# Three halves of an up projection from plain products to seven block products, and sums of a later weight made earlier

## The chip, the cores and the metric

The kernel runs on one core of one Trainium2 chip. A core has TensorE (PE, matrix products), VectorE (DVE), ScalarE (ACT), GpSimd (POOL) and SyncE (SP), which run independently and wait for each other through semaphores. Transfers are issued in this kernel from two queues, SP's and POOL's; only POOL's can add to what lies at the destination. An engine works through its own instructions in order, so a waiting instruction holds back all behind it on that engine.

The metric is the device time of one execution in microseconds. Lower is better.

## The reference

One encoder layer over 512 tokens of width 2048, in float32:

```python
h = rms_norm(x, pre_mix_g)
z = h @ w_in                                   # [q | k | v | u], 1024 columns each
a = chunked_attention(q, k, v, rel_bias)       # 8 heads of 128
p = multiscale_pool(u, pool_w, pool_scale)     # 4 groups of 256, windows 2, 4, 8, 16
x = x + rms_norm(concat(a, p) @ w_o, post_mix_g)
h = rms_norm(x, pre_ffn_g)
up = causal_dwconv(h @ w_up, conv_w, conv_b)   # 2048 -> 2 x 5632, 3 taps over tokens
y = (gelu(up[:, :5632]) * up[:, 5632:]) @ w_down
x = x + rms_norm(y, post_ffn_g)
```

## The kernel before

**Products.** Every float32 operand is split in two parts of a shorter format, hi and lo (`split`, L133: ACT rounds, L135; DVE subtracts, L136), and a product is hi*hi + hi*lo + lo*hi: three matmuls with 128x512 operands (`mm3`, L150).

**Stages on PE**, with where they lie in the profiled execution: the heads' q, k and v and the attention (0 to 303 us); the *pool branch*, that is eight projections u0 to u7 of 128 channels each, with the trailing means (`pool_proj`, `pool_keep`, `pool_mix`; 303 to 406 us); the product with w_o, by seven block products instead of eight (`wo_product`; 406 to 564 us); the up projection (564 to 1443 us); the product with w_down, again by seven block products (to 1877 us). `pool_keep` (L485) clears small margins on POOL before DVE's additions over them.

**Up projection.** It is done in 22 units of 256 channels. A unit has two halves: p = 0 feeds the gelu (`gate`), p = 1 is the value that it is multiplied with (`product`, which stores g to DRAM by POOL's queue). The first `PLAIN` = 3 units are plain (`up`, L984): 16 blocks of the inner dimension, two of 128 channels, three matmuls each. The weights come in four tiles per half. Of these, the first unit is written out (its second half reads the tiles `w10_0` to `w10_3`).

From unit 3 on each half is a *pair* k = 0, 1, ... (k counts halves) of `seven` products P1 to P7 (L1185): the 2 x 2 blocks of channels and inner dimension, against the 2 x 2 blocks of inner dimension and tokens, by a scheme that needs seven block products for eight. A block product is `mm2` (L156): eight matmuls of 512 columns (hi of the weight against hi and lo of h) and eight of 256 (lo of the weight against hi of h). On the side of h, P1, P2, P4 and P7 read blocks of h where they lie (for P7 a block must first be overwritten by a difference: `h_difference`, L1056); P5, P6 and P3 read sums made by `h_sums` (L1033) into tiles h5, h6, h3. On the side of w_up, the factors of P5, P6 and P4 are made in one buffer `x` in turn, that of P7 in the buffer `y` of P3: after a factor is split, POOL's queue adds the next block of w_up to its buffer (`add`, L1100), and so on:

```python
if i == 1 and k not in self.alone:
    self.add(k, "x", 1, 0)
elif i == 5:
    self.add(k, "x", 1, 1)
elif i == 6:
    self.add(k, "x", 0, 1)
elif i == 3:
    self.add(k, "y", 1, 0)
```

P1 of a pair is split from `x` too before the first addition; only for the first and the last pair (`alone`) does it have a buffer `w` of its own, and `x` is loaded and added to separately. In the steady order two neighbouring pairs are interleaved: place 7 k + (0, 2, 4, 6, 8, 10, 12) for P1, P2, P5, P3, P6, P7, P4. The first and the last few products have an order of their own (`begin`, `end`). Factors are split up to four products ahead of PE (`AHEAD`; the tiles `w4` hold four hi and lo pairs, shared with the plain weights), and loaded up to six further (`RAW`). The buffers `x` lie in a ring of four (`raw_x`), which `h_sums` also uses for its temporaries, two of which live until `h_difference`. `raw4` is a ring of five for the other raw weights.

**Sums in DRAM.** Seven block products with w_o and w_down need sums of their blocks. `sums_in_dram` (L296) makes them with transfers from DRAM to DRAM: `copy` by SP's queue, behind the last weight load issued so far, and `add` by POOL's queue. It has 32 steps for w_o and then 16 for w_down (eight copies, eight adds, 1 MB each; tiles `t`); in w_down's, the sums come in the order 5, 7, 6, 4, where 6 starts as a copy of the finished 5 and 4 as a copy of the finished 6. The rest of the kernel takes single steps at places written out: 24 during the heads, eight in the pool branch, seven in `wo_product` and nine in `up`.

**Order.** The order of PE's instructions is the program's (`manual_schedule`). On the other engines and queues a planner places each instruction when the kernel is built, by its own estimates of when operands and buffers are ready, with earlier instructions of the program preferred; `issue_after(ins)` makes an instruction follow `ins` on the same engine. A tile name with `bufs=n` is a ring of n buffers; a new use waits until the old one is no longer read. PSUM is a ring of eight banks.

Of the kernel before, what the change touches and what calls it, by code (L numbers as in the profile page):

```python
# [75 lines left out]
def encoder_layer(ctx: ExitStack, tc: tile.TileContext, x, xT, vecs, rel, post_mix, post_ffn,  # L76
# [56 lines left out]
    def split(hi, lo, src, scale=None):  # L133
        if scale is None:
            rounded = nc.scalar.activation(hi, src, AF.Copy)  # L135
            rest = nc.vector.tensor_sub(lo, src, f32(hi))  # L136
        else:
            rounded = nc.scalar.activation(hi, src, AF.Copy, scale=scale)
            rest = nc.vector.scalar_tensor_tensor(lo, src, scale, f32(hi), op0=ALU.mult, op1=ALU.subtract)
        split.last, split.rest = rounded.ins, rest.ins  # L140
        return rounded.ins
# [138 lines left out]
    for i in WO:  # L280
        for cc in range(2):
            specs += wo_specs(i, cc)
        if i == 1:
            specs += pm_spec(3)
    for u in range(PLAIN):
        for p in range(2):
            specs += [(f"w{p}{u}_{i}", w_up[u, p, :, i // 2, :, i % 2 * 512:(i % 2 + 1) * 512].rearrange(
                "m p c -> p m c"), 2, 512) for i in range(4)]

# [69 lines left out]
    with tc.tile_pool(name="p1", bufs=2, reuse_waits="tile") as p1:  # L359
# [39 lines left out]
        def project(name, between=None):  # L399
            ps = bank(name)  # L400
            for i in range(2):
                if i and between:
                    between()
                w = weights.get(f"{name}_{i}")
                for j in range(8):
                    kb = 8 * i + j
                    mm3(ps, part(w, j), blk(hT, kb), kb == 0, kb == KD - 1)
            return ps
# [73 lines left out]
        def pool_proj(g, j):  # L482
            pool_keep(g, j, project(f"u{2 * g + j}"))
# [53 lines left out]
        for h in range(2, HEADS):  # L537
# [9 lines left out]
            else:  # L547
                values(h - 2)
            next(sums_step)
        next(sums_step)  # L550
        pool_proj(0, 0)
        turn(6)
        scores(7)
        pool_proj(0, 1)
        next(sums_step)
        values(6)
        next(sums_step)
        pool_proj(1, 0)
        next(sums_step)
        turn(7)  # L560
        pool_proj(1, 1)
        next(sums_step)
        values(7)
        mixT += [acc8(f"mixT{i}", "B").rearrange("p (a b) -> p a b", a=4) for i in (2, 3)]
        pool_mix(0, keep_mix)
        next(sums_step)
        pool_proj(2, 0)
        next(sums_step)
        pool_proj(2, 1)
        pool_mix(1, keep_mix)  # L570
        next(sums_step)
        pool_proj(3, 0)
        u7 = project("u7")


# [16 lines left out]
        def wo_product(i, cc, left, between=None):  # L592
            ps = [bank(f"m{i}{cc}{t}") for t in range(2)]
            if cc:
                next(sums_step)
            for q in range(4):
                w = weights.get(f"wo{i}_{cc}_{q}")
                for j in range(2):
                    kb = 2 * q + j
                    for t in range(2):  # L600
                        mm3(ps[t], tuple(v[:, kb, t * P:(t + 1) * P] for v in left), part(w, j), kb == 0, kb == 7)
                if between:
                    between(q)
            return ps
# [335 lines left out]
    with tc.tile_pool(name="p3", bufs=2, reuse_waits="tile") as p3:  # L940
# [37 lines left out]
        def normed(ps):  # L978
            z = new_z()
            for j in range(2):  # L980
                nc.vector.tensor_mul(z[:, j, :], ps[j], R)
            return z

        def up(u, p, between=()):  # L984
            ps = [bank(f"up{u}_{p}_{j}") for j in range(2)]
            between = list(between)
            for i in range(4):
                w = weights.get(f"w{p}{u}_{i}")
                factors.prefetch(4 - len(weights.specs) + weights.used)
                for kb in range(4 * i, 4 * i + 4):  # L990
                    for j in range(2):
                        mm3(ps[j], part(w, j, slice(kb % 4 * P, (kb % 4 + 1) * P)), g_both(hT, kb),
                            kb == 0, kb == KD - 1)
                step = between.pop(0) if between else None
                if step:
                    step()
                next(sums_step, None)
            return ps

        def spread2():  # L1000
# [27 lines left out]
        def raw_x(name):  # L1028
            return p3.tile([P, 1024], F32, tag="x", bufs=4, name=name)
# [31 lines left out]
        class Factors:  # L1061
# [1 line left out]
            RAW, AHEAD = 10, 4  # L1063

            def __init__(self):
                n = 2 * (NU - PLAIN)

                self.alone = 0, n - 1  # L1070
                place_of = {1: 0, 6: 8, 2: 2, 7: 10, 5: 4, 4: 12, 3: 6}
                begin = [(0, 1), (0, 5), (0, 2), (0, 3)]
                end = [(n - 1, 5), (n - 2, 6), (n - 1, 3), (n - 1, 1), (n - 2, 7), (n - 1, 6), (n - 2, 4),
                       (n - 1, 7), (n - 1, 2), (n - 1, 4)]
                order = sorted((7 * k + at, k, i) for k in range(n) for i, at in place_of.items())
                self.order = begin + [(k, i) for _, k, i in order if (k, i) not in begin + end] + end
                self.raw, self.made, self.loaded, self.used = {}, [], 0, 0

            def block(self, k, m, kh):
                return w_up[PLAIN + k // 2, k % 2, m, kh]  # L1080

            def load(self, k, i):
                def raw(what, tile_, m, kh):
                    nc.sync.dma_start(tile_, self.block(k, m, kh))
                    self.raw[k, what] = tile_

                if i == 1 and (k, "w") not in self.raw:
                    raw("w" if k in self.alone else "x", raw_x("wx"), 0, 0)
                elif i == 5 and k == self.alone[0]:
                    raw("x", raw_x("wx"), 0, 0)  # L1090
                    self.add(k, "x", 1, 0)
                elif i == 5 and k == self.alone[1]:
                    raw("w", raw_x("wx"), 0, 0)
                    raw("x", raw_x("wx"), 1, 0)
                elif i == 3:
                    raw("y", raw4("wy"), 1, 1)
                elif i == 2:
                    raw("z", raw4("wz"), 0, 1)
# [4 lines left out]
            def make(self, k, i):  # L1103
                what = {1: "w" if k in self.alone else "x", 3: "y", 7: "y", 2: "z"}.get(i, "x")
                v = self.raw[k, what]
                if (k, i) == (self.alone[1], 5):
                    nc.vector.tensor_add(v, v, self.raw[k, "w"])
                hi, lo = w4("wfh"), w4("wfl")
                split(hi, lo, v)
                if i == 1 and k not in self.alone:  # L1110
                    self.add(k, "x", 1, 0)
                elif i == 5:
# [5 lines that stand above are left out]
                self.made.append(tuple(v.rearrange("p (a b) -> p a b", a=8) for v in (hi, lo)))  # L1118
# [52 lines left out]
        def keep_all(k):  # L1171
            one, m, a = zs.pop((k, "1")), zs.pop((k, "m")), banks.pop((k, "a"))
            z = new_z()
            nc.vector.tensor_add(z[:, 0, :T], one[:, 0, 0], one[:, 0, 1])
            nc.vector.tensor_add(z[:, 1].rearrange("p (a b) -> p a b", a=2), m[:, :, 0], m[:, :, 1])
            nc.scalar.activation(z[:, 0, T:], a[:, T:], AF.Copy)
            nc.vector.tensor_add(z[:, 0, T:], a[:, :T], z[:, 0, T:])
            nc.vector.tensor_mul(flat(z), flat(z), flat(RR))
            u = PLAIN + k // 2
            if k % 2:  # L1180
                product(u, gates.pop(u), z)
            else:
                gates[u] = gate(u, z)
# [8 lines left out]
        def first_left():  # L1192
# [4 lines left out]
            split(hi, lo, v)  # L1197
            return hi, lo

        z = up(1, 0, [spread2, lambda: product(0, gate(0, normed(ups[0])), normed(ups[1]))])  # L1200
        a = gate(1, normed(z))
        z = up(1, 1, [lambda: h_sums(0)])
        product(1, a, normed(z))
        z = up(2, 0, [None, lambda: h_sums(1)])
        a = gate(2, normed(z))
        z = up(2, 1)
        h_difference()
        product(2, a, normed(z))
        rights, firsts = [right(0, cc) for cc in range(2)], []
        for r in rights:  # L1210
            next(r)
# [8 lines left out]
        for k, i in factors.order:  # L1220
            seven(k, i)
            keep(k, i)
            if (k, i) == (end, 6):
                summed.close()
                pr = ctx.enter_context(tc.tile_pool(name="pr", bufs=2, side="right", reuse_waits="tile"))
            if (k, i) == (end, 6):
                next_first()
            elif (k, i) == (end - 1, 4):
                next_first()
# [248 lines left out]
```

## Time and profile before

| | us |
|---|---|
| median of three runs | 1877.95 (1877.62 to 1878.02) |
| the profiled execution, its own time | 1878.27 |
| its span | 1876.5 |
| PE busy | 1864.2 (99%) |
| DVE busy | 1418.1 (76%) |
| ACT busy | 1002.3 (53%) |

The profile shows one execution. Times of instructions are in us from the start of the span, an instruction's row names the line of the kernel (a helper's line where a helper issues it), the operation and the tiles it writes and reads; in brackets stands how long its engine was idle before it, and what ended that. "L135 ACT ... x152 | 161.0, 1060 | 119.9" is a group: 152 instructions, 161.0 us busy in all, 1060 ns each, 119.9 us of idle time before them. Matmuls overlap in the pipeline, so the rate of PE is read from the distance of starts. SPq is SP's queue; the row of a transfer shows its issue, and its landing is given separately. TensorE's granted clock was 0.999 of full speed over the execution.

### The profile page before, as it was taken

The numbers are of one execution on the slowest core, as the hardware profiler recorded it, in microseconds if no ns is written. First come the engines' busy times: TensorE is split into PE (matmuls) and PEld (weight loads), VectorE is DVE, ScalarE is ACT, GpSimd is POOL, SyncE is SP. The second block draws the span as 40 slices with busy tenths as digits, with TensorE's granted clock in tenths as the row PEclk, the third lists the DMA queues.
The fourth block names the chain that finished last, engine by engine and source line by source line (L and its number), as shares of the span: only waits on it lengthen the run. The fifth ranks groups of instructions, "written<-read, shape, count | busy, mean of one in ns | idle before, by whom it ended". The sixth has DMA issues, their size and how long they took to land.

```text
span 1876.5 us, 24700 instructions
## 1 busy us (share of the span) xinstructions
PE 1864.2 (99%) x9438; PEld 1592.8 (85%) x9438; DVE 1418.1 (76%) x1607; ACT 1002.3 (53%) x1263; POOL 287.1 (15%) x388
## 2 busy tenths in 40 slices
PE   9999999999999999999999999999999999999998
PEld 7888888888889888888888888888888888888886
DVE  5555444677598767888878888888887899899886
ACT  6433333346455345656656566565665665565553
POOL 4301011000000102122121211212121011111101
PEclk9999999999999999999999999999999999999999
DMA  8899599449797848889888898888979967877785
GB/s 287 254 246 243 163 259 241 112 141 330 221 302 252 228 146 192 201 201 204 200 199 206 204 204 200 201 203 207 204 180 291 352 226 176 203 202 176 176 233 156
DMA packets 181990, 404.47 MB, mean 216 GB/s; under 512 B 11312, under 2 KB 62384, under 8 KB 176560
## 3 DMA queue, kind: packets, MB, share of 16 engines
q0 software_dynamic: 50384, 150.49, 41.9%
q1 hardware_dynamic: 131488, 252.41, 39.9%
q8 instruction: 74, 1.21, 0.3%
q14 instruction: 44, 0.36, 0.1%
HBM read 356.72 MB, written 96.47 MB: 242 GB/s over the span
## 4 chain that ended last, share of the span: by engine, by line
PE 97%; DVE 1%; DMA 1%; ACT 1%; issue 0%; SPq 0%; POOL 0%; DVEq 0%; POOLq 0%; ACTq 0%
PE qa L159 15%; PE qa L165 8%; PE qg L159 7%; PE pa L151 4%; PE pa L154 4%; PE pa L153 4%; PE qg L165 4%; PE qd L159 4%; PE m L151 3%; PE m L153 3%; PE m L154 3%; PE up L153 2%; PE up L154 2%; PE up L151 2%; PE pg L151 2%; PE pg L154 2%
## 5 line engine op out<-in xcount | busy, mean ns | idle before, releaser
L159 PE MATMUL qa<-gT,wfh 128*128 128x512 f32 x912 | 228.3, 392 | 0.0
L136 DVE TENSOR_TENSOR wfl<-wx,wfh 128x1024 fp32r<-128x1024 f32 x152 | 185.9, 1223 | 54.3 <-ACT wfh L135 40.0
L135 ACT ACTIVATE wfh<-wx 128x1024 fp32r<-128x1024 f32 x152 | 161.0, 1060 | 119.9 <-PE qg L159 43.8
L159 PEld LDWEIGHTS qa<-gT,wfh 128*128 128x128 f32 x912 | 164.1, 189 | 29.4
L1101 POOL DMA_DIRECT2D wx<-in_w_up x113 | 96.9, 857 | 463.4 <-DVE wfl L136 422.5
L159 PE MATMUL qg<-h,wfh 128*128 128x512 f32 x608 | 150.2, 389 | 0.0
L136 DVE TENSOR_TENSOR bl<-b,bh 128x2048 fp32r<-128x2048 f32 x56 | 127.0, 2287 | 18.1 <-ACT bh L135 11.7
L135 ACT ACTIVATE bh<-b 128x2048 fp32r<-128x2048 f32 x56 | 106.1, 1913 | 60.5 <-DVE b L864 25.2
L159 PEld LDWEIGHTS qg<-h,wfh 128*128 128x128 f32 x608 | 113.9, 188 | 23.6
L135 ACT ACTIVATE wfh<-wy 128x1024 fp32r<-128x1024 f32 x76 | 80.6, 1060 | 93.4 <-PE qg L159 48.9
L165 PE MATMUL qa<-gT,wfl 128*128 128x256 f32 x912 | 127.7, 283 | 0.9 <-ACT zm L1162 0.9
L151 PE MATMUL pa<-bh,ah 128*128 128x512 f32 x320 | 124.5, 389 | 0.0
L153 PE MATMUL pa<-bl,ah 128*128 128x512 f32 x320 | 124.5, 389 | 0.0
L154 PE MATMUL pa<-bh,al 128*128 128x512 f32 x320 | 124.5, 389 | 0.0
L165 PEld LDWEIGHTS qa<-gT,wfl 128*128 128x128 f32 x912 | 119.9, 191 | 4.2 <-ACT zm L1162 1.1
L136 DVE TENSOR_TENSOR wfl<-wy,wfh 128x1024 fp32r<-128x1024 f32 x76 | 92.8, 1221 | 5.2 <-ACT wfh L135 2.8
L136 DVE TENSOR_TENSOR wfl<-wz,wfh 128x1024 fp32r<-128x1024 f32 x38 | 46.6, 1227 | 55.2 <-PE qa L159 52.2
L165 PEld LDWEIGHTS qg<-h,wfl 128*128 128x128 f32 x608 | 82.9, 190 | 5.9
L165 PE MATMUL qg<-h,wfl 128*128 128x256 f32 x608 | 84.8, 282 | 0.0
L932 POOL DMA_DIRECT2D sum<-part x30 | 36.2, 1206 | 262.0 <-DVE part L918 192.7
L159 PE MATMUL qa<-h,wfh 128*128 128x512 f32 x304 | 76.1, 392 | 0.0
L159 PE MATMUL qd<-gT,wfh 128*128 128x512 f32 x304 | 75.1, 389 | 0.0
(543 smaller groups left out, 4697.8 us busy)
## 6 DMA issues: line engine op xcount, KB each, us to landing
wx<-in_w_up POOLq DMA_DIRECT2D x113, 512.0 KB, 6.4
b<-in_w_down SPq DMA_DIRECT2D x32, 1024.0 KB, 6.9
wx<-in_w_up SPq DMA_DIRECT2D x40, 512.0 KB, 5.6
wz<-in_w_up SPq DMA_DIRECT2D x38, 512.0 KB, 5.9
wy<-in_w_up SPq DMA_DIRECT2D x38, 512.0 KB, 4.6
wy<-in_w_up POOLq DMA_DIRECT2D x38, 512.0 KB, 6.9
sum<-part POOLq DMA_DIRECT2D x38, 512.0 KB, 7.9
wt<-in_w_o POOLq DMA_DIRECT2D x16, 1024.0 KB, 11.9
```

Of the source, the lines that this page charges most:

```text
L135: rounded = nc.scalar.activation(hi, src, AF.Copy)
L136: rest = nc.vector.tensor_sub(lo, src, f32(hi))
L151: nc.tensor.matmul(ps, l[0], r[0], start=first, stop=False, skip_group_check=onto)
L153: nc.tensor.matmul(low, l[0], r[1], start=False, stop=False, skip_group_check=onto)
L154: nc.tensor.matmul(ps, l[1], r[0], start=False, stop=last, skip_group_check=onto)
L159: nc.tensor.matmul(ps, w[0][:, kb], pairs[kb][0], start=fresh and not kb, stop=last, skip_group_check=not fresh)
L165: nc.tensor.matmul(ps[:, sl], w[1][:, kb], pair[:, sl], start=False, stop=last, skip_group_check=not fresh)
L932: nc.gpsimd.dma_start(dest, v, accum_op=ALU.add)
L1101: nc.gpsimd.dma_start(self.raw[k, what], self.block(k, m, kh), accum_op=ALU.add)
```

## The change

Plain work now ends after the first half of the second unit: `PLAIN` = 3 counts halves, so two halves of unit 0 and the gelu half of unit 1 stay plain, and the value half of unit 1 and both halves of unit 2 join the pairs (41 instead of 38). The first products are P1 and P2 of the pairs 0 and 1, then P5 and P3 of pair 0; after them comes the steady order. The buffer `w` of pair 0 moves to the ring `raw4`. `h_sums` stands ahead of `up(1, 0)` in the program instead of inside two of the plain halves, and `h_difference` behind the first product, with its splits following the split of the third factor on ACT and on DVE.

The steps of `sums_in_dram` are taken in twos and threes in the pool branch (23 there instead of eight), one more in `wo_product`, and none in `up`, so that all 16 of w_down's sums but one add are issued in the pool branch.

```diff
-    for u in range(PLAIN):
-        for p in range(2):
+    for n in range(PLAIN):
+        for u, p in (divmod(n, 2),):
             specs += [(f"w{p}{u}_{i}", w_up[u, p, :, i // 2, :, i % 2 * 512:(i % 2 + 1) * 512].rearrange(
...
-        next(sums_step)
+
+        def more_sums(n):
+            for _ in range(n):
+                next(sums_step, None)
+
+        more_sums(2)
         pool_proj(0, 0)
         turn(6)
         scores(7)
         pool_proj(0, 1)
-        next(sums_step)
+        more_sums(2)
         values(6)
-        next(sums_step)
+        more_sums(2)
         pool_proj(1, 0)
-        next(sums_step)
+        more_sums(2)
         turn(7)
         pool_proj(1, 1)
-        next(sums_step)
+        more_sums(3)
         values(7)
         mixT += [acc8(f"mixT{i}", "B").rearrange("p (a b) -> p a b", a=4) for i in (2, 3)]
         pool_mix(0, keep_mix)
-        next(sums_step)
+        more_sums(3)
         pool_proj(2, 0)
-        next(sums_step)
+        more_sums(3)
         pool_proj(2, 1)
         pool_mix(1, keep_mix)
-        next(sums_step)
+        more_sums(3)
         pool_proj(3, 0)
+        more_sums(3)
         u7 = project("u7")
...
             if cc:
-                next(sums_step)
+                more_sums(1)
...
                 if step:
                     step()
-                next(sums_step, None)
             return ps
...
-                n = 2 * (NU - PLAIN)
+                n = 2 * NU - PLAIN
...
-                begin = [(0, 1), (0, 5), (0, 2), (0, 3)]
+                begin = [(0, 1), (0, 2), (1, 1), (1, 2), (0, 5), (0, 3)]
...
-                return w_up[PLAIN + k // 2, k % 2, m, kh]
+                return w_up[(PLAIN + k) // 2, (PLAIN + k) % 2, m, kh]
...
-                    raw("w" if k in self.alone else "x", raw_x("wx"), 0, 0)
+                    raw("w" if k in self.alone else "x", raw4("wx") if k == self.alone[0] else raw_x("wx"), 0, 0)
...
                 split(hi, lo, v)
+                if len(self.made) == 2:
+                    self.third = split.last, split.rest
...
-            u = PLAIN + k // 2
-            if k % 2:
+            u, p = divmod(PLAIN + k, 2)
+            if p:
                 product(u, gates.pop(u), z)
...
+        for i in range(2):
+            h_sums(i)
         z = up(1, 0, [spread2, lambda: product(0, gate(0, normed(ups[0])), normed(ups[1]))])
-        a = gate(1, normed(z))
-        z = up(1, 1, [lambda: h_sums(0)])
-        product(1, a, normed(z))
-        z = up(2, 0, [None, lambda: h_sums(1)])
-        a = gate(2, normed(z))
-        z = up(2, 1)
-        h_difference()
-        product(2, a, normed(z))
+        gates[1] = gate(1, normed(z))
...
             seven(k, i)
             keep(k, i)
+            if (k, i) == factors.order[0]:
+                with ExitStack() as behind:
+                    for ins in factors.third:
+                        behind.enter_context(tc.issue_after(ins))
+                    h_difference()
```

## The prediction

> **What bounds the kernel now.** I read the head of the page first, then the chain that ended last, then what PE waited for.
>
> ```profile
> span 1876.5 us, 24700 instructions
> PE 1864.2 (99%) x9438; PEld 1592.8 (85%) x9438; DVE 1418.1 (76%) x1607; ACT 1002.3 (53%) x1263; POOL 287.1 (15%) x388
> PE 97%; DVE 1%; DMA 1%; ACT 1%; issue 0%; SPq 0%; POOL 0%; DVEq 0%; POOLq 0%; ACTq 0%
> PE qa L165 <- ACT zm L1162: 0.9, 1, 0.9
> PE up L153 <- DVE gT L139: 0.6, 1, 0.6
> ```
>
> TensorE is busy for 99% of the span, 97% of the final chain is its matmuls, and in the middle it idles twice, for 0.9 and 0.6 us. So every microsecond of matmuls taken out is a microsecond of time, as long as the other engines and the queues still deliver on time; every new wait of PE costs its full length. Two prices follow: what the exchanged matmuls save, and what the moved work makes PE wait.
>
> **Part 1: three plain halves become seven-product halves.** A plain half (`up`) is 16 blocks x 2 x 3 = 96 matmuls of 512 columns; one with seven products (`seven`) is 7 x 8 of 512 and 7 x 8 of 256. A busy PE overlaps its instructions, so I take periods between starts. The first matmuls of three successive plain halves, and then the same step of two pairs in the steady stretch:
>
> ```profile
> 636.31 0.39 PE L151 MATMUL up<-gT,w_0h 128*128 128x512 f32 x1
> 658.07 0.39 PE L151 MATMUL up<-gT,w_0h 128*128 128x512 f32 x1
> 679.83 0.39 PE L151 MATMUL up<-gT,w_0h 128*128 128x512 f32 x1
> 852.30 1.91 PE qa L165 x16
> 1378.62 1.91 PE qa L165 x16
> ```
>
> A plain half takes 21.76 us (0.227 per matmul). Between 852.30 and 1378.62 lie 27 pairs: 526.32 / 27 = 19.49 us each, 2.785 per product. The three halves (second unit's value half, both halves of the third) therefore give 3 x (21.76 - 19.49) = 6.8 us. This is the whole gain that I can see.
>
> Their other work has cover. Three halves shed 12 plain weight splits and six multiplications by R, and take on 21 factor splits, 12 accumulating loads on POOL's queue, nine loads on SP's instead of twelve, and the additions of `keep`. That is the steady stretch's work, and there PE stays full:
>
> ```profile
> 702.00:1430.00 728.00, 727.14 (x4179) 642.03 (x4179) 600.34 (x705) 442.13 (x540) 158.13 (x190) 1.00 0.87 198
> 596.00:642.00 46.00, 46.00 (x207) 38.10 (x206) 44.24 (x47) 20.18 (x21) 5.43 (x4) 1.00 0.74 212
> 642.00:660.00 18.00, 18.00 (x81) 14.93 (x80) 4.44 (x7) 3.26 (x4) 2.38 (x3) 1.00 0.84 218
> ```
>
> (PE, PEld, DVE, ACT, POOL busy, clock, DMA share.) DVE is busy 600.34 / 728 = 82% there; more of the same costs nothing.
>
> **Part 2: the start of the products.** They begin at 636.31 instead of 701.59, right behind a stretch in which DVE is 44.24 of 46 us busy. What fills it is `h_sums`, then the first unit's `product`:
>
> ```profile
> 595.97 3.49 DVE L1037 TENSOR_TENSOR q<-gT 128x1024 f32<-128x1024 f32 x3
> 634.20 1.22 DVE L136 TENSOR_TENSOR h<-q,h 128x1024 fp32r<-128x1024 f32 x1
> 641.80 0.69 DVE L968 TENSOR_TENSOR ca<-ca,cb 128x512 f32<-128x512 f32 x1
> 657.53 1.52 ACT L944 ACTIVATE ca<-z,vec 128x512 f32<-128x512 f32 x2 [14.74 <-DMA gd<-ca]
> 648.01 0.91 POOL L1101 DMA_DIRECT2D wx<-in_w_up  x1 [10.96 <-DMA wx<-in_w_up]
> L135 ACT ACTIVATE wfh<-wx 128x1024 fp32r<-128x1024 f32 x152 | 161.0, 1060 | 119.9 <-PE qg L159 43.8
> L136 DVE TENSOR_TENSOR wfl<-wx,wfh 128x1024 fp32r<-128x1024 f32 x152 | 185.9, 1223 | 54.3 <-ACT wfh L135 40.0
> DMA to landing us min/median/max: 3.6/6.0/10.5
> wx<-in_w_up SPq DMA_DIRECT2D x40, 512.0 KB, 5.6
> 625.43 0.39 PE L151 MATMUL up<-gT,w_2h 128*128 128x512 f32 x1
> ```
>
> (The landing times are those of `wx` from 700 to 1430 us; the row below them gives KB and median landing of its plain loads.) The sums already run there; traced ahead of `up(1, 0)` they go ahead of the first unit's multiplications by R instead of between them, and end some 6 us sooner (three additions and a split of 1.14 us, and gaps), near 628. The same DVE work fits before 642 as now.
>
> The new order is P1 P2 of pair 0, P1 P2 of pair 1, then P5 P3 P6 P7 of pair 0, P5 of pair 1, P4 of pair 0. At 2.785 us each, P5 stands at 647.4, P6 at 653.0, P7 at 655.8, P4 at 661.4. The first four need no sum of h, so 11 us cover `h_sums`; PE does not wait there.
>
> But P6's factor is P5's buffer plus a block that POOL's DMA accumulates, and may be loaded only when P5's factor has been split. In the steady order P6 stands four products behind P5, 11.1 us; here two. P5's split cannot start before the buffers of pair 0's first factor are free, at 636.3 + 2.8 = 639.1. In the best case: split 1.06 + 1.22 to 641.5, issue 0.3, landing 6.0, split 2.3: 650.1, nearly 3 us early. I do not expect the best case. P5's raw tile shares a ring of four with the temporaries of `h_sums` (free near 628); load (5.6 us), accumulation (6.0) and issue give 641; DVE still has the first unit's product until about 642.3 and the second unit's multiplication by R (1.2), so P5's split ends near 644.7. The stores of g stand in POOL's queue ahead of P6's accumulation; another 1 us. Then 644.7 + 0.3 + 7 + 2.3 = 654.3: PE waits 1.3 us for P6. P4 depends on P6 alike, three products behind: 654.3 + 8.6 = 662.9 against 661.4 + 1.3: 0.2 to 0.6 more. I take 1.9 us, and as bounds 0 (best case above) and 6 (landings of 10.5 instead of 6 at P6, and part of it at P4).
>
> The Trainium skill, DMA: Bandwidth & Descriptors, section on the anatomy of one DMA on the GpSimd path, fits such a transfer as 2.0 us plus bytes over 436 GB/s, an estimate of 3.2 us for 512 KB. By it P6's factor would be ready near 650.5 and the wait would be zero; the row's 6.0, with none under 3.6, disagrees, and I go by the row.
>
> Edits that I cost at nothing: `h_difference` (two splits, 4.6 us of ACT and DVE) moves behind the third factor's split; P7 at 655.8 needs it, gT's quarter is free once `up(1, 0)` reaches its third weight tile, 625.43 above, and cover is gone only if DVE lags by 10 us. P1 of pair 0 in a `raw4` tile rather than the ring of four avoids a wait for the sums. The stores of `product(0)` (ACT's 14.74 us wait above) come sooner, since no add of w_down stands before them; ACT's wait for `ca` should shrink to some 8 us, with two or three factors split ahead.
>
> **Part 3: the sums of w_down move.** Before, eight copies on SP and eight adds on POOL, 1 MB each, start from 407.66 to 635.90; now they go behind loads of the pool branch, and the last copy of w_o's sums moves up by one load.
>
> ```profile
> 331.00:395.00 64.00, 64.00 (x293) 53.31 (x292) 36.38 (x61) 20.96 (x30) 1.06 (x12) 1.00 0.38 107
> 100.00:180.00 80.00, 80.00 (x390) 67.80 (x389) 44.10 (x86) 29.41 (x58) 8.98 (x18) 1.00 1.03 261
> 407.66 0.60 SPq L300 DMA_DIRECT2D t<-in_w_down  x1
> 635.90 1.16 POOL L303 DMA_DIRECT2D t<-in_w_down  x1 [5.65 <-DMA t<-t]
> t<-in_w_down POOLq DMA_DIRECT2D x8, 1024.0 KB, 13.9
> t<-t SPq DMA_DIRECT2D x8, 1024.0 KB, 9.7
> 331.31 0.37 SPq L146 DMA_DIRECT2D u_0r<-in_w_in  x1
> 370.89 0.37 SPq L146 DMA_DIRECT2D wo_0r<-in_w_o  x1
> 325.60 1.25 POOL L303 DMA_DIRECT2D wt<-in_w_o  x1 [15.85 <-DMA wt<-wt]
> 327.05 0.29 DVE L452 TENSOR_REDUCE nm<-s 128x1 f32<-128x128 f32 x1 [6.65 <-POOL u L488]
> 395.00:410.00 15.00, 15.00 (x68) 12.43 (x67) 14.90 (x20) 10.41 (x12) 0.40 (x4) 1.00 0.32 98
> ```
>
> Room is there: the DMA share is 0.38 from 331 to 395, and from 100 to 180 the same kind of copies and adds ran at 1.03 with PE at 80.00 of 80. The first copies go behind the load at 331.31, the last behind the one at 370.89. Each chain is copy, add, copy, add, copy, about 10 + 14 + 10 + 14 + 10 us, so the last add starts near 389, a little after its place. Behind a waiting copy on SP stand weight loads; behind a waiting add on POOL stand the memsets of `pool_keep`, for which DVE waits, with the weight splits behind it: at 325.60 to 327.05 an add waited 15.85 us, DVE lost 6.65, PE nothing. In the pool branch a split runs three weight tiles of 24 matmuls ahead (3 x 24 x 0.227 = 16 us), so holds of 10 to 15 us are covered. I take 0; bounds 0 and 12. Where the adds leave (410 to 640) PE did not wait for them, so nothing is won.
>
> **Sum.** 1878.27 us of the profiled execution (0.3 over the median, 1.8 over its span) - 6.8 + 1.9 + 0 = 1873.4; from the median 1877.95, 1873.0.
>
> **The rivals.**
> First, everything is hidden: P5's accumulation lands early and DVE is free, as in the best case; nothing in the rows excludes 3.6 us landings. 1877.95 - 6.8 = 1871.1. The skill's fit above is this rival.
> Second, the start costs more: `ca` of the second unit, in ACT's order ahead of the factors, is held as in the row of 14.74 us. With P3 due at 650.2, `ca` released at 652 and 1.5 us of its own, then a split (2.3), P3 waits 5.6 us: 1871.1 + 5.6 = 1876.7. For it speaks that the planner misjudged exactly this wait before; against it that POOL then stood 10.96 us before the store, behind w_down's traffic.
> Third, on the other side: the pool branch's adds hold POOL past 395. From there DVE has no slack (14.90 of 15 us), and w_o's weight tiles last only 12 matmuls, so splits run 3 x 2.7 = 8.2 us ahead. A hold of 21 us on a memset of `pool_keep` costs 21 - 8.2 = 12.8: 1871.1 + 12.8 = 1883.9. It decides from a hold of 8.2 + 6.8 + 3.8 = 18.8 us, when the gain is gone and 0.2% lost. For it: two chained transfers share each queue, so the second half's chain may end near 402. Against it: 325.60 above.
>
> **How the numbers follow.** Forecast (waits of 1 to 3 us in all, 1872 to 1874.2) 0.38; all hidden (1870.3 to 1872, one steady hiccup of 0.9 more or less) 0.17; start dear (1874.2 to 1881) 0.25; pool branch (over 1881) 0.15; anything else slower 0.05. 0.2%, about what a measurement of this kernel can tell from no change, is 3.8 us: faster means under 1874.2. So faster 0.55, same 0.25, slower 0.20. The likeliest two alone span 1870.3 to 1874.2; to hold 8 in 10 the range goes up to 1880.5.
>
> **What would show it.** Right: `seven` from about 636, 41 periods of 19.49, one or two idle gaps of PE before P6 and P4 of pair 0 (some 653 and 662 us), released by a split whose chain runs through `wx`; no `t` transfers after 430, DMA share near 1 from 331 to 395, PE full there. Wrong: an idle PE at `u` or at the first `m` between 370 and 430, or gaps before P3 released by ACT's `ca`, or a steady period other than 19.49.

## The result, and the profile after

The changed kernel takes 1887.22 us (median of 6 runs, 1886.54 to 1891.61), the kernel before in the same comparison 1877.70 (6 runs, 1876.13 to 1878.02): a ratio of 1.0058, with a 95% interval of 1.0045 to 1.0071. It is slower by half a per cent where I had forecast a quarter of a per cent faster. The profiled execution took 1887.21, with a span of 1885.4.

The head of the page, the shares of the final chain and the list of what PE waited for, all of the changed kernel:

```profile
span 1885.4 us, 24890 instructions
PE 1862.0 (99%) x9486; PEld 1591.7 (84%) x9486; DVE 1438.4 (76%) x1631; ACT 1019.2 (54%) x1287; POOL 297.3 (16%) x400
PE 92%; DMA 3%; DVE 2%; issue 1%; ACT 1%; SPq 0%; POOL 0%; POOLq 0%; DVEq 0%; ACTq 0%
...
PE qg L159 <- ACT zb L1165: 6.0, 1, 6.0
PE u L151 <- ACT u_1h L135: 1.5, 1, 1.5
PE m L153 <- DVE wo_2l L136: 1.4, 1, 1.4
PE u L154 <- DVE u_1l L136: 1.3, 2, 0.8
...
PE m L151 <- ACT wo_2h L135: 1.1, 1, 1.1
...
PE qa L165 <- ACT zm L1169: 0.7, 1, 0.7
```

PE still shows 99% busy, and this is the first thing to learn here: the busy time fell by only 2.2 us although the seven products save 6.8. Of the missing 4.6 us, about 3.0 are matmuls that run at a lowered clock behind two of the waits (1.6 us behind the first in the list and 1.4 around 418 us); they are longer and count as busy. Where the rest lies I did not trace. The share by itself tells nothing; the list of waits and the distances between stages do.

The distances between the first matmuls of four stages, in the profiled executions of the two kernels (us):

| | before | after | difference |
|---|---|---|---|
| pool branch and w_o (first `u` to first `up`) | 261.8 | 270.7 | +8.9 |
| up projection (first `up` to first `pa`) | 878.9 | 879.3 | +0.4 |
| product with w_down (first `pa` to the end) | 433.0 | 433.4 | +0.4 |

So there are two questions: what costs 8.9 us where only DMAs were added, and where the 6.8 us of the up projection went.

**The pool branch.** The busy times by stretch, of the kernel before and then of the changed one (PE, PEld, DVE, ACT, POOL, with the number of instructions; granted clock; DMA share; GB/s):

```profile
370.00:395.00 25.00, 25.00 (x112) 20.68 (x112) 14.35 (x22) 7.30 (x9) 0.49 (x6) 1.00 0.33 106
410.00:430.00 20.00, 20.00 (x90) 16.58 (x89) 17.63 (x20) 9.83 (x12) 1.16 (x1) 1.00 0.94 271
```

```profile
331.00:370.00 39.00, 39.00 (x183) 32.58 (x182) 17.44 (x28) 10.95 (x17) 4.79 (x6) 1.00 1.07 260
370.00:395.00 25.00, 23.02 (x101) 18.42 (x100) 7.83 (x12) 4.96 (x6) 2.71 (x7) 1.00 1.07 262
395.00:410.00 15.00, 14.19 (x63) 11.44 (x62) 9.87 (x15) 4.95 (x6) 2.88 (x8) 1.00 0.94 230
410.00:430.00 20.00, 17.06 (x67) 13.21 (x66) 20.00 (x26) 11.18 (x13) 0.20 (x2) 0.91 0.71 205
```

The matmul counts say it best: 101 instead of 112, 63 instead of 68 (the row of before for 395 to 410 stands in the prediction) and 67 instead of 90, 39 fewer; times 0.227 us that is 8.9. Until 370 nothing is lost, though the DMA share is already 1.07. Then DVE does 12 operations where it did 22. What it waits for, and what holds POOL and the loads, in the timeline of the changed kernel:

```profile
371.48 1.16 POOL L303 DMA_DIRECT2D t<-in_w_down  x1 [17.56 <-DMA t<-t]
...
375.52 0.64 POOL L495 MEMSET us<- 128x1 f32 x1
376.19 1.52 DVE L493 TENSOR_TENSOR us<-us 128x526 f32<-128x526 f32 x2 [5.69 <-POOL us L495]
386.82 1.06 ACT L135 ACTIVATE u_1h<-u_1r 128x1024 fp32r<-128x1024 f32 x1 [7.56 <-DMA u_1r<-in_w_in]
397.99 1.16 POOL L303 DMA_DIRECT2D t<-in_w_down  x1 [19.23 <-DMA t<-t]
399.29 0.70 DVE L493 TENSOR_TENSOR us<-us 128x524 f32<-128x524 f32 x1 [5.93 <-POOL us L495]
```

Two things happen together. An add of w_down stands on POOL until its copy has landed, 17.56 and 19.23 us; the memsets of `pool_keep` are behind it, and DVE waits 5.69 and 5.93 us for them, with the weight splits behind. And the loads of `u` come late: between 331 and 410 us their median landing is 28 us, where before it was 4 (the row of the kernel before, then two of the changed kernel):

```profile
u_0r<-in_w_in SPq DMA_DIRECT2D x3, 512.0 KB, 4.0
u_0r<-in_w_in SPq DMA_DIRECT2D x2, 512.0 KB, 28.2
364.52 17.61 SPq L146 DMA_DIRECT2D u_1r<-in_w_in  x1
```

The last row is an issue on SP's queue that itself took 17.61 us, where the row of the same load took 0.37 in the kernel before; all that stands behind it on SP had to wait. What held it the trace does not tell.

**The start of the products.** The chain of work of the changed kernel from 651 to 676 us, in order of time (start, length, what):

```profile
651.85 8.07 DMA wy<-in_w_up
...
660.99 0.35 ACT wfh L135
...
661.93 1.50 ACT ca L950 x2
663.44 0.49 ACT zb L1165
...
663.97 3.55 PE qg L159 x8
...
671.30 0.61 ACT zm L1169
...
671.95 1.22 PE qa L165 x8
```

P5 ended at about 657.9. P3 comes next and sums into the same PSUM bank (`BANK`: 5 and 3 both "g"), so ACT must first copy P5 out of it (`zb`, L1165, 0.5 us of work). On ACT's queue that copy stood behind the split of P7's factor, which waited for an accumulating load (8.07 us), another split, and two `ca` of unit 1's gate. PE stood for 6.04 us, and P3's first eight matmuls then took 3.55 us (granted clock 0.56 from 664 to 667.5 us); P1's first eight took 1.98:

```profile
643.83 1.98 PE L159 MATMUL qa<-gT,wfh 128*128 128x512 f32 x8
```

The balance closes to 0.4 us: 878.9 - 6.8 (the gain) - 0.9 - 0.6 (two pauses of PE that the kernel before had, in the steady stretch and in the first unit) + 6.0 + 0.7 (the two waits) + 1.6 (the slower matmuls) = 878.9, measured 879.3.

### The profile page after: what moved, and what is told of

It reads as the page before. It is cut to its first block, busy times and chain, and to the rows that moved or that the text cites. A ratio compares the mean times of both kernels' runs of the same rounds, so it can differ in the third digit from the quotient of the medians.

```text
span 1885.4 us, 24890 instructions
## 1 busy us (share of the span) xinstructions
PE 1862.0 (99%) x9486; PEld 1591.7 (84%) x9486; DVE 1438.4 (76%) x1631; ACT 1019.2 (54%) x1287; POOL 297.3 (16%) x400
## 4 chain that ended last, share of the span: by engine, by line
PE 92%; DMA 3%; DVE 2%; issue 1%; ACT 1%; SPq 0%; POOL 0%; POOLq 0%; DVEq 0%; ACTq 0%
PE qa L159 16%; PE qa L165 8%; PE qg L159 8%; PE qg L165 4%; PE pa L151 4%; PE pa L154 4%; PE pa L153 4%; PE qd L159 4%; PE m L153 2%; PE m L154 2%; PE m L151 2%; PE qd L165 2%; PE pg L151 2%; PE pg L154 2%; PE pg L153 2%; PE v L153 2%
## 5 line engine op out<-in xcount | busy, mean ns | idle before, releaser
L135 ACT ACTIVATE wfh<-wx 128x1024 fp32r<-128x1024 f32 x164 | 173.7, 1059 | 137.6 <-PE qg L159 52.5
L159 PE MATMUL qa<-gT,wfh 128*128 128x512 f32 x984 | 246.4, 392 | 0.0
L136 DVE TENSOR_TENSOR wfl<-wx,wfh 128x1024 fp32r<-128x1024 f32 x164 | 200.5, 1222 | 57.7 <-ACT wfh L135 43.6
L159 PEld LDWEIGHTS qa<-gT,wfh 128*128 128x128 f32 x984 | 177.0, 189 | 31.7
L1106 POOL DMA_DIRECT2D wx<-in_w_up x122 | 104.6, 860 | 509.4 <-DVE wfl L136 447.0
L159 PE MATMUL qg<-h,wfh 128*128 128x512 f32 x656 | 163.6, 392 | 6.0 <-ACT zb L1165 6.0
L159 PEld LDWEIGHTS qg<-h,wfh 128*128 128x128 f32 x656 | 124.0, 189 | 32.0 <-ACT zb L1165 6.2
L165 PE MATMUL qa<-gT,wfl 128*128 128x256 f32 x984 | 137.8, 283 | 0.7 <-ACT zm L1169 0.7
L165 PEld LDWEIGHTS qa<-gT,wfl 128*128 128x128 f32 x984 | 129.4, 191 | 4.6 <-ACT zm L1169 1.3
L136 DVE TENSOR_TENSOR wfl<-wy,wfh 128x1024 fp32r<-128x1024 f32 x82 | 100.1, 1220 | 8.6 <-PE qa L159 2.9
```

Source lines behind the costliest of these rows:

```text
L159: nc.tensor.matmul(ps, w[0][:, kb], pairs[kb][0], start=fresh and not kb, stop=last, skip_group_check=not fresh)
L165: nc.tensor.matmul(ps[:, sl], w[1][:, kb], pair[:, sl], start=False, stop=last, skip_group_check=not fresh)
L1106: nc.gpsimd.dma_start(self.raw[k, what], self.block(k, m, kh), accum_op=ALU.add)
```

## Experiments

All runs were timed against the kernel before. "Up" below is the distance from the first `up` to the first `pa`, "pool" that from the first `u` to the first `up`, as in the table above.

### The two halves of the change by themselves

e1 is the kernel before with only the sums moved; e2 is the changed kernel with the sums at their old pace:

```diff
 # e1: the kernel before, with the changed kernel's pool branch, and
             if cc:
-                next(sums_step)
+                more_sums(1)
...
-                next(sums_step, None)
 # e2: the changed kernel, one sum at a time in the pool branch as before, and
+            more_sums(1 + (q == 3))     # in the second half of the first unit, after each weight tile
...
+                more_sums(1)            # after each weight tile of up(1, 0)
```

> The kernel before with only the sums moved: 23 steps in the pool branch, one in wo_product, none in up; the up projection as before. Theory A (the two parts of the change cost independently): the loss between the first matmul of u and the first of up that the changed kernel shows, 262.2 to 270.7 us, some 8.5 to 9, appears here alone, about 1886.5 us, with PE idle behind u_1 and wo splits between 385 and 420 and its clock lowered behind them. Theory B (the loss in the pool branch comes only together with the new start of the products, through another placement by the planner): under 1880.

> The changed kernel with the sums of w_down at their old pace: eight steps in the pool branch, seven in wo_product, and the nine of up in the second half of the first unit (five) and in up(1, 0) (four). Theory A: the pool branch is as before, no idle PE there; the start of the products keeps its 6.0 us wait before P3, so 6.8 saved less 6.7 of waits and 1.7 of lowered clock and plus 0.9 of a pause in the steady stretch that went: 1877.7 to 1879. Theory B: the adds that now end beside the first accumulations make P3, P6 and P7 wait longer, over 1882.

e1: 1885.06 (1883.84 to 1887.9), ratio 1.0044 (1.0029 to 1.0059); pool 271.5, up 878.6. The moved sums alone cost what the change loses in the pool branch, here mostly in one wait:

```profile
PE u L154 <- DVE u_1l L136: 5.5, 1, 5.5
```

e2: 1881.81 (1880.20 to 1884.09), ratio 1.0025 (1.0015 to 1.0036); pool 261.9, as before, but up 879.7. The seven products alone do not gain either: their wait is still there in full, 5.99 us. The places are those of theory A, but the time is 2.8 us above its range; the profiled execution is the fastest of the eight (1880.20), and where the others lose more no trace shows.

### What in the pool branch costs the time

e4 clears the margins of `pool_keep` on DVE, so that nothing on POOL stands behind an add; e8 takes the sums out of the pool branch again and packs them into the product with w_o (10 in the pool branch, 14 in w_o, none in the up projection):

```diff
 # e4
-            nc.gpsimd.memset(u[:, :PAD], 0.0)
+            nc.vector.memset(u[:, :PAD], 0.0)
...
-                    nc.gpsimd.memset(nxt[:, :step], 0.0)
+                    nc.vector.memset(nxt[:, :step], 0.0)
 # e8: one sum at a time in the pool branch as before, two more at its end, and in wo_product
...
             if cc:
-                more_sums(1)
+            more_sums(1)
```

> The changed kernel with the margins of the trailing means (memsets of u and us in pool_keep) cleared by DVE instead of POOL, so that nothing in pool_keep stands behind POOL's waiting adds. Theory H (POOL's hold is what reaches PE, through DVE): DVE's two waits of 5.7 and 5.9 us for us go, and PE's waits at 401 and 412 to 418 with the lowered clock behind them; 1887.2 - 4 = 1883 or less, and only the wait at 388 stays. Theory L (the late loads of u, 28 us from issue to landing, set the lag by themselves): the times stay within 1.5 us of 1887.2 and PE idles at the same places.

> The changed kernel with the sums of w_down at another pace: two more of them in the pool branch than before (at its end), two per wo_product pair instead of one, none in up. Theory P (it is the pace in the pool branch, two to three steps for each projection, that holds POOL and delays the loads of u): u to up takes 262 to 264 us as before instead of 270.7, so about 1887.2 - 7 = 1880, the wait before P3 staying. Theory R (the 16 sums cost PE the same wherever they are packed into less than their old 230 us): 1885 or more, with idle PE in the product with w_o.

e4: 1881.69 (1878.57 to 1883.76), ratio 1.0021 (1.0012 to 1.0031): 5.5 us less for moving some memsets. In the profile the pool distance falls by 7.2, to 263.5, and the up distance rises by 1.5, to 880.8: there PE waited 6.40 us before P3, and the slower matmuls behind it cost 2.6. The stretch from 370 to 395 us:

```profile
370.00:395.00 25.00, 25.00 (x112) 20.72 (x111) 10.14 (x18) 6.03 (x7) 2.31 (x2) 1.00 1.11 276
```

PE is full although the DMA share is as high as in the changed kernel and the loads of `u` still land late:

```profile
u_0r<-in_w_in SPq DMA_DIRECT2D x2, 512.0 KB, 26.8
```

So at this traffic, with loads of `u` landing 19 to 28 us after issue, the pool branch of e4 does not stop PE: they use up the lead of the splits, and the hold of POOL did most of the rest. One wait of the changed kernel is not explained by this. PE's 1.5 us at 388 was for a split that waited for its load alone; that load was out for 28 us in the changed kernel (issued at 358.93) and for 19 in e4 (360.02 to 379.0), and why it lands sooner there no run shows.

e8: 1888.63 (1888.14 to 1890.04), ratio 1.0060 (1.0045 to 1.0075), pool 269.5. The pool branch is whole again, and the product with w_o loses it:

```profile
430.00:500.00 70.00, 65.04 (x277) 51.05 (x276) 43.04 (x39) 37.82 (x46) 4.63 (x4) 1.00 1.02 317
wo_0r<-in_w_o SPq DMA_DIRECT2D x2, 512.0 KB, 17.4
```

In the same stretch of the kernel before these loads landed in 9.9 us. No memset holds DVE there; ACT's splits of `wo_0r` and `wo_1r` wait for their loads, and loads landing 17 us after issue are enough, since a w_o tile lasts only 12 matmuls. The sums cost nothing over the 230 us in which they ran; packed here, the product with w_o pays for them.

### Where the gain of the seven products went

Each of the next runs takes one suspect away. e3 lets DVE make the copy `zb` of pair 0; e5 puts a product of pair 1 between P5 and P3; e6 gives P3 of pair 0 a PSUM bank of its own, so that it needs no copy; e7 is e6 with the sums at their old pace:

```diff
 # e3
-                nc.scalar.activation(zs[k, "5"], banks[k, "g"], AF.Copy)
+                if k:
+                    nc.scalar.activation(zs[k, "5"], banks[k, "g"], AF.Copy)
+                else:
+                    nc.vector.tensor_copy(zs[k, "5"], banks[k, "g"])
 # e5
-                begin = [(0, 1), (0, 2), (1, 1), (1, 2), (0, 5), (0, 3)]
+                begin = [(0, 1), (0, 2), (1, 1), (0, 5), (1, 2), (0, 3)]
 # e6, e7
+            own = (k, i) == (0, 3)
+            at = "h" if own else BANK[i]
-            if i in FIRST:
+            if i in FIRST or own:
...
                 nc.vector.tensor_add(v, banks.pop((k, "g")), v)
+                if k == 0:
+                    nc.vector.tensor_add(v, banks.pop((k, "h")), v)
```

> The changed kernel, but for pair 0 the copy of P5's result out of PSUM is done by DVE instead of ACT. Theory Q (P3 waits because this copy stands on ACT behind splits that wait for accumulating loads, not for P3's own factor): the 6.0 us idle before P3 falls to under 2.5 and the lowered clock behind it goes, 1887.2 - 5 = 1882, down to 1879. Theory F (the factors themselves are late, the copy only came last): the same time is lost before P6 or P7, 1886 or more.

> The changed kernel with P5 of pair 0 one place earlier, so that P2 of pair 1 stands between P5 and P3. Theory K (P3 waits because it accumulates into the PSUM bank from which P5's result must first be copied out, and the copy stands behind splits that wait for accumulating loads): the copy becomes ready 2.8 us before P3 is due and is placed ahead of those splits; the 6.0 us wait before P3 falls below 2 and the lowered clock goes: 1887.2 - 6 = 1881. Theory F (the accumulated factors are late in any case): the wait moves to P6 or P7, 1885 or more.

> The changed kernel with a PSUM bank of its own for P3 of pair 0 (added in by one more DVE addition of 0.7 us behind P6), so that P3 does not wait for the copy of P5. The order of the products is the changed kernel's. Theory K: the 6.0 us before P3 go, PE's next wait is at P6 or P7, at most 1.5 us, and the clock stays up: 1887.2 - 6.5 = 1880.7. Theory F: PE waits as long at P3, P6 or P7 together, 1885 or more.

> The bank of its own for P3 of pair 0, with the sums of w_down at their old pace (as in the run with seven products alone). Theories A and K together: no idle PE in the pool branch, at most 1.5 us at the start of the products; the whole 6.8 us of matmuls come through less that: 1877.6 - 6.8 + 1.5 = 1872.3, faster than the kernel before. If something else costs in the seven products, over 1876.

e3: 1886.86, ratio 1.0055 (1.0040 to 1.0070). e5: 1887.98, ratio 1.0052 (1.0035 to 1.0069). e6: 1886.92, ratio 1.0048 (1.0033 to 1.0063). e7: 1879.55, ratio 1.0010 (1.0000 to 1.0019). e7's median is 2.3 under e2's, but its profiled span, 1878.0, is only 0.4 under (1878.4); the profiled execution of e5 is its slowest (1893.09). None of the four is below the kernel before, and where the wait went is in their lists of PE's waits, one fence for each of e3, e5 and e6:

```profile
PE qg L159 <- DVE zb L1168: 5.9, 1, 5.9
```

```profile
PE qa L165 <- ACT zm L1169: 4.5, 1, 4.5
PE qg L159 <- ACT zb L1165: 3.5, 1, 3.5
```

```profile
PE qa L165 <- ACT zm L1169: 6.6, 2, 6.0
```

DVE is no better a place for the copy, since the subtractions of the same waiting splits are in its queue. A product in between makes two waits out of one; before the second, ACT had stood 6.75 us at `ca` of unit 1's gate, for the store of unit 0 that still read the buffer. A bank for P3 moves the wait to P7, which sums into P6's bank and waits for that copy (`zm`), again behind work in ACT's queue: a split that waited 1.85 us for its load, another split and the gelu. After these four I could not tell two causes apart: the accumulating loads are simply too late for this order, or they are in time and only the copies, in ACT's order, are not.

e9 and e10 (changed kernel, and e2) were to tell these apart. They leave order and banks alone and force ACT's order: the splits of the factors at places 6 to 8 behind the copy `zb`, those at places 9 to 11 behind P7's `zm`:

```diff
+                with tc.issue_after(self.behind) if 6 <= len(self.made) <= 11 else nullcontext():
-                split(hi, lo, v)
+                    split(hi, lo, v)
...
-                self.prefetch(n)
+                self.prefetch(n, min(3, self.used - 2) if 3 <= self.used <= 8 else 0)   # so many fewer splits ahead
...
-                nc.scalar.activation(zs[k, "5"], banks[k, "g"], AF.Copy)
+                copied = nc.scalar.activation(zs[k, "5"], banks[k, "g"], AF.Copy)
+                if k == 0:
+                    factors.behind = copied.ins    # and the same at zm of P7
```

> The changed kernel with the same begin and the same PSUM banks; only ACT's order at the start of the products is another: the splits of the factors at places 6 to 8 (P6, P7 of pair 0, P5 of pair 1) stand behind the copy zb of P5, and those at places 9 to 11 behind the copy zm of P7, instead of ahead of them. In the trace of the changed kernel P5 ended at about 657.8 and the split of P6's factor could start at 657.45 and that of P7's at 660.02, when their accumulating loads had landed. Theory S (ACT's order is the cause: what PE lacks is the copy, which a split that waits for a load holds up; the factors themselves are in time): zb ends at about 658.5, P3 waits 0.7 to 1.3 instead of 6.04, P6 and P7 wait under 1.5 each, the lowered clock behind the wait goes too; together 5 to 7 less, 1880.5 to 1882.5. Theory L (the accumulating loads are late by themselves, two places do not cover 7 to 8 us): the wait moves to P6 or P7 with 4 to 6 and the time stays within 1.5 of 1887.

> The seven products with the sums at the old kernel's places, and ACT's order as in the run beside it. Theory S: the seven products alone then keep their gain: 1878.4 to 1881.8 less 5 to 7, that is 1871.5 to 1876, faster than the kernel before by 1 to 6. Theory L: 1878 to 1881, as without the other order.

e9: 1891.55 (1889.17 to 1895.10), ratio 1.0075 (1.0060 to 1.0090); e10: 1884.93 (1884.07 to 1887.16), ratio 1.0040 (1.0028 to 1.0053). Both worse, against both theories. ACT's timeline in e9 shows why the wait before P3 was still 5.25 us:

```profile
658.98 1.52 ACT L950 ACTIVATE ca<-z,vec 128x512 f32<-128x512 f32 x2 [8.15 <-DMA gd<-ca]
660.41 0.57 ACT L1166 ACTIVATE zb<-qg 128x512 f32<-128x512 f32 x1
```

With the splits gone, the next in the queue held the copy: `ca` writes a buffer that the store of unit 0 still reads (8.15 us idle), as e5 could have told me. The holder that I had removed was not the only one. And a second wait of 3.24 us came before P7 of pair 1. I put it down to holding back the splits at places 9 to 11; no run tests that by itself. e11 (on e2) and e12 (on e4) drop that hold and put the gate of unit 1 behind the split of P7's factor:

```diff
+                with tc.issue_after(self.behind) if len(self.made) in (6, 7, 8) else nullcontext():
...
-        gates[1] = gate(1, normed(z))
+        z1 = normed(z)
...
+            if (k, i) == (0, 6):
+                with tc.issue_after(factors.eighth):    # the split of the factor at place 7
+                    gates[1] = gate(1, z1)
```

> The seven products with the sums at the old kernel's places. On ACT nothing that waits for a transfer stands ahead of the copy zb of P5 any more: the splits of the factors at places 6 to 8 stand behind it, and so do the two operations ca of unit 1's gate, which in the two runs before waited until the store of the buffer they write had landed (ACT idle 8.5 with the releaser DMA gd<-ca). The splits at places 9 to 11 are where the planner puts them. Theory S2 (the holders of ACT stand in line: split, split, ca; the copy itself can run when P5 ends): zb runs within 1 of P5's end, the wait before P3 falls from 5.6 to under 1.3, those before P6, P7 and P4 stay under 2 each, no lowered clock behind them: 1872 to 1876.5, below the kernel before. Theory L (late loads): a wait of 4 or more stays in places 5 to 9, 1878 to 1883.

> The changed kernel with both repairs: the margins of the trailing means cleared on DVE (which took 5.5 off by itself, 1881.69) and the order of ACT of the run beside it. Theory S2: another 5 to 7 less, 1874.5 to 1877.5, about the time of the kernel before. Theory L: 1880 to 1885.

e11: 1875.66 (10 runs, 1873.74 to 1877.45) against 1877.78, ratio 0.9986 (0.9977 to 0.9995); up 874.9. e12: 1876.11 (1874.04 to 1878.99), ratio 0.9992 (0.9982 to 1.0001); pool 262.2, up 874.7. Both lie in the ranges of theory S2. ACT and PE at the same place in e11:

```profile
649.59 0.60 ACT L1169 ACTIVATE zb<-qg 128x512 f32<-128x512 f32 x1 [4.98 <-PE qg L165]
...
652.68 1.06 ACT L135 ACTIVATE wfh<-wy 128x1024 fp32r<-128x1024 f32 x1 [1.49 <-DMA wy<-in_w_up]
654.01 1.53 ACT L950 ACTIVATE ca<-z,vec 128x512 f32<-128x512 f32 x2 [0.27 <-DMA gd<-ca]
...
664.91 1.06 ACT L135 ACTIVATE wfh<-wx 128x1024 fp32r<-128x1024 f32 x1 [2.78 <-DMA wx<-in_w_up]
665.87 0.58 ACT L1169 ACTIVATE zb<-qg 128x512 f32<-128x512 f32 x1
```

```profile
650.24 2.12 PE L159 MATMUL qg<-h,wfh 128*128 128x512 f32 x8 [0.69 <-ACT zb L1169]
657.01 1.21 PE L165 MATMUL qa<-gT,wfl 128*128 128x256 f32 x8 [0.91 <-ACT zm L1175]
666.50 2.11 PE L159 MATMUL qg<-h,wfh 128*128 128x512 f32 x8 [0.87 <-ACT zb L1169]
```

At P3 of pair 0, ACT now waits for PE, not PE for ACT's queue. Same products, same banks, same loads: the accumulating loads were in time, and all but 0.7 of the 6 us was the order of one engine's queue, with two kinds of holders in line. Three waits of 0.7 to 0.9 remain. The first is the copy itself; the second, before P7, is the copy and 0.3 us of a split that was under way; the third, before P3 of pair 1, is again a copy behind a split that waited 2.78 us for its load, though the product in between covers most of that delay.

e12's median lies 0.45 us above e11's, less than the spread of either, so that no cost of the moved sums is visible once POOL has no memsets for DVE behind them; no gain is visible either. e11 is the only version with an interval below 1, by 2.1 us or 0.11% between medians; that is less than the 0.2% that I called measurable, and I claim no more for it. Its profile shows 4.0 us less in the up projection, but the profiled execution (1873.83) is among the fastest of the ten; where the others lose part of it no trace shows.

## Why the prediction was wrong

**Part 1, the gain of 6.8: right.** The same step of the pairs in the chain of the changed kernel:

```profile
704.67 1.91 PE qa L165 x16
1386.94 1.91 PE qa L165 x16
```

35 periods in 682.27 us, 19.49 each, as before. That the steady stretch carries three more pairs at no cost was right too. That the pause of 0.9 which the kernel before had there is gone is luck: e8 has one of 0.87 us at 1414 and e12 one of 1.13 at 1244.

**Part 2, the start at 1.9 (bounds 0 and 6): wrong in place and size.** The step that failed is "PE waits 1.3 us for P6": PE waited 6.04 us for P3, and not for a factor. What I worked out of the sums of h and P6's factor was good or pessimistic: moved by the 8.1 us that the stage came later, `h_sums` was to end at 636, and ended at 636.7; P5's split at 652.8, ended at 649.8; P6's factor at 662.4, was ready at 659.8, before its turn at 660.5 (643.8 + 6 x 2.785). The two splits on DVE, in the timeline of the changed kernel:

```profile
648.59 1.23 DVE L136 TENSOR_TENSOR wfl<-wx,wfh 128x1024 fp32r<-128x1024 f32 x1 [0.51 <-ACT wfh L135]
658.54 1.22 DVE L136 TENSOR_TENSOR wfl<-wx,wfh 128x1024 fp32r<-128x1024 f32 x1 [3.15 <-ACT wfh L135]
```

The addition took 7.3 us from issue to landing and P7's `wy` 8.07; the Trainium skill, DMA: Bandwidth & Descriptors, section on the anatomy of one DMA on the GpSimd path, would give an estimate of 3.2, and these rows disagree once more. But I followed only the factors. I never asked what P3 needs besides its factor: the bank that `BANK` gives to P5 as well, and so a copy on ACT, behind whatever ACT's order puts first. P3 and P7 are the second products in banks that P5 and P6 have just used; in the steady order another product stands between such two, in the new start none. The cost was 6.0 + 0.7 of waits and 1.6 of slower matmuls, 8.3 instead of 1.9 and outside the bounds; the sum had no term for slower matmuls behind a wait. The second rival had the engine, the product and nearly the size (P3 waits 5.6, ACT held by `ca`); its road, through P3's factor, was another, so its nearness in size is partly luck. Its holder shows as such in e5 and e9; in the changed kernel the waiting splits stood ahead of it.

**Part 3, the sums at 0 (bounds 0 and 12): wrong by 8.9.** The step that failed is "holds of 10 to 15 us are covered". The holds were 17.56 and 19.23. Behind the first stood a copy of 1 MB that took 19.1 us from issue to landing where I had taken 10; the copy behind the second took 8.1, but was issued only at 389.32, behind loads whose issues took 4.2 and 2.4 us on SP, although the add that it needs had landed at 384.55. And the cover of 16 us, three weight tiles ahead, was spent by the loads themselves, landing 28 us after issue. I had compared with 100 to 180 us, where the same DMA share cost PE nothing; e4 bears this out for the traffic, and what the comparison left out were the memsets behind the adds. The third rival named the mechanism, POOL held and DVE behind its memsets, at a price of 12.8 us; by itself, in e1, it cost 7.5 (1885.06 against 1877.57). "The last add starts near 389" was 400.2, with the one before it at 398.0.

**The chances.** I gave the second and the third rival 0.25 and 0.15 and treated them as alternatives. They lie in different stages and use different queues, so both could come, and did: 1871.1 + 5.6 + 12.8 = 1889.5 by the prediction's own numbers, against 1887.2. The range had to take in that sum. Part 3 had no gain to give, only a price; its expected value could not be 0 with a bound of 12.

**What would show it.** The signs were well chosen: idle PE at `u` and at the first `m` between 370 and 430, and a gap before P3 released by ACT; the releaser's name alone was another (`zb` in place of `ca`). The transfers of `t` did end in time, and the DMA share did go to 1.07; that was no sign of success.

## What to carry to other kernels

When products are reordered, write down for each not only the operand that it reads but the bank that it writes and the instruction that must empty that bank first; then look at what stands ahead of that instruction in its own engine's queue. An instruction of half a microsecond behind one that waits for a DMA costs the DMA's lateness, and removing one holder may only show the next, so read the queue until it is free, before trying banks and orders. Small work on a queue that also issues waiting DMAs (memsets behind adds) belongs on another engine before more DMAs go on that queue; and rivals from different stages are added, not chosen between.

## What the runs showed of the hardware

PE's matmuls were slower behind long waits. After 6.04 us of idle time, eight matmuls of 512 columns took 3.55 us instead of 1.98, and after 5.25 in e9, 3.78; after 0.69 in e11, 2.12. In the profiles of all these kernels, each of the fifteen waits of 3.24 us or more was followed by such matmuls, at 1.4 to 2.7 us of extra time. For shorter waits the runs show no such rule. Around 418 us in the changed kernel PE waited 1.05 us, did one matmul and waited 1.41 again; the next ones are spaced at 0.43 us, and 2.7 us later at 0.23:

```profile
416.45 0.49 PE L151 MATMUL m<-wo_2h,a 128*128 128x512 f32 x1 [1.05 <-ACT wo_2h L135]
418.35 0.80 PE L153 MATMUL m<-wo_2l,a 128*128 128x512 f32 x1 [1.41 <-DVE wo_2l L136]
418.94 0.63 PE L154 MATMUL m<-wo_2h,a 128*128 128x512 f32 x1
419.37 0.63 PE L151 MATMUL m<-wo_2h,a 128*128 128x512 f32 x1
```

The Trainium skill, TensorE: Matmul & The Clock Gate, section "What's actually happening", says that the clock is halved after an idle window of about 3.4 us. The waits of 5 to 6 us agree with it; the two short ones here, 2.5 us together, were enough as well, and so was one of 2.03 us in e9. But the same two waits at the same place in e3 (1.05 and 1.42) and in e5 (1.02 and 1.41) were followed by matmuls at 0.23 us, and so was one of 2.79 us in e5; what decides between them no run shows. For a sum of costs it means that a wait of PE of 3.2 us or more had a price of its own on top in these kernels, 1.6 us in the changed one.
